# Three products instead of two while the stream comes in, and the sum of squares moved from GpSimd to ACT and DVE

## The chip, the cores and the metric

One core of one Trainium2 chip runs the whole program. The metric is device time in microseconds, the median of several executions. A separate profiled execution gives the page and the trace that are quoted.

## The reference

A two-layer decoder trunk on 512 tokens of 1024 numbers, in float32. Layer 0 mixes with a gated linear recurrence (HGRN2) in eight heads, layer 1 with differential attention; after each stands a gated feed-forward block with a short convolution. The change touches the very beginning of layer 0:

```python
def rmsnorm(x, g):
    x32 = x.astype(jnp.float32)
    y = x32 * lax.rsqrt(jnp.mean(x32 * x32, axis=-1, keepdims=True) + EPS)
    return (y * g.astype(jnp.float32)).astype(x.dtype)

def hgrn2_mixer(h, w_in, w_out, g_norm, lb):
    proj = h @ w_in
    q, f, i, g = jnp.split(proj, [HG_FDIM, 2 * HG_FDIM, 3 * HG_FDIM], axis=-1)
    q = jax.nn.silu(q)
    log_f = jnp.logaddexp(jnp.log(lb), jnp.log1p(-lb) + jax.nn.log_sigmoid(f))
    k = -jnp.expm1(log_f)
    ...
    o = rmsnorm(o, g_norm) * jax.nn.silu(g)
    return o @ w_out
```

Each head has four products with the normalised input: f (forget), q, i (the values, called V here) and g (the output gate). The mean square of x is needed for every token before any of them can be used; since it is a factor for a whole token, the products run on x times the gain, and the factor is applied to the result.

## The kernel before

Activations lie transposed: eight tiles x0 to x7 of 128 features by 512 tokens. Every float32 product is made of three matmuls (mm3, L99 to L104): an operand is split into a high part (ACT, L57 for weights, L60 for x) and a low part (DVE, L58 and L61), and high x high, low x high and high x low are added up. A product of one head's f, q or g is thus 8 k-tiles of 3 matmuls of 512 columns, 24 in all, into one PSUM bank of the tag mm, of which there are four. V is made for two heads at once from two weights of 512 KB (w_i), in four chunks of 128 tokens, each 24 matmuls of 256 columns into a bank of mm.

Weights come by SyncE's queue (SP, L79) into three staging buffers (wst), in the order in which the program issues them; SP waits at an issue until its buffer has been split. The split weights whi and wlo have three buffers each.

begin (L226 to L271) is written out by hand (manual_schedule) for TensorE, DVE, ACT and GpSimd. The x tiles and the first two weights (f and q of head 0), the latter in four pieces of 1, 2, 3 and 2 k-tiles, come in turns. For each k-tile x is split, then the pieces that have come, then three matmuls of f and three of q run. Beside it the sum of squares is made: GpSimd squares tiles 0 to 3 and adds them (L262, L265, L266), ACT squares tiles 4 to 7 (L243), DVE adds those (L245) and joins both sums (L268, L269).

Behind it come sums (L181: the sum over features, by TensorE with a tile of ones), rstd on DVE (L191 and L158 to L164, which ends in rcol) and TensorE's L186, which turns rcol into a tile rb that ACT copies (L198). V is evacuated with rcol (ACT, L320), f and q with rb (DVE, L327 and L337, fe and qe).

After begin the order of hgrn is not written by hand: a scheduler orders the instructions of each engine ahead of time, by what it thinks each lasts. The loop over heads has prep (from fe and qe to the decayed q and k of all levels, on DVE and ACT), values (V), intra (scores within a chunk: TensorE L412 to L426 into the bank at; transposes of k L434, copied by ACT L436 as kt; states kt x V L439; masks on DVE L457; readout products L479 and L481), gate (L486 to L489: g times rb is ge, its sigmoid sg, the product gg) and readout. gate(0) runs in the loop at head 2, on project(2), the product with weight number 2.

At head 2 bias_vector makes the table of relative biases for the attention much later: a matmul (L708), a subtraction on DVE (L709) and a write of 1024 rows of 383 numbers to a buffer in HBM, bdram, by SP's queue (L711). It stands among the weights on that queue.

Of the kernel before, what the change touches and what calls it, by code (L numbers as in the profile page):

```python
# [11 lines left out]
F32 = mybir.dt.float32  # L12
F32R = mybir.dt.float32r
I32 = mybir.dt.int32
AF = mybir.ActivationFunctionType
ALU = mybir.AluOpType
# [3 lines left out]
P = 128  # L20
T = 512
D = 1024
KD = D // P
# [11 lines left out]
class Trunk:  # L35
# [187 lines left out]
        return self.gains[:, which, n:n + 1]  # L223


    def begin(self, xs, acc, f_ps, q_ps):  # L226

        tc, nc, a = self.tc, self.nc, self.a
        v, s, pool = nc.vector, nc.scalar, nc.gpsimd
        raw = [self.wp.tile([P, 1024], F32, tag="wst", name="wst", bufs=3) for _ in range(2)]  # L230
        parts = [self.weight_tiles() for _ in range(2)]
        for k in range(KD):
            nc.sync.dma_start(self.x[k], a["x_t"][k])
            if k in PIECES:
                c = slice(k * P, PIECES[k] * P)
                for i in range(2):
                    nc.sync.dma_start(raw[i][:, c], a["w_fqg"][i][:, c])
        half = KD // 2
        sqs = [self.sp.tile([P, T], F32, tag="sq", name="sq", bufs=2) for _ in range(2)]
        acc2 = self.sp.tile([P, T], F32, tag="res", name="acc2", bufs=1)  # L240

        def squares(n):
            s.activation(acc2 if n == half else sqs[n % 2], self.x[n], AF.Square)  # L243
            if half < n < KD - 1:
                v.tensor_tensor(acc2, acc2, sqs[n % 2], ALU.add)  # L245

        with tc.manual_schedule(engines=ORDERED):
            warm = self.bank("at")
            for _ in range(WARM):
                nc.tensor.matmul(warm[:, 0:P], self.ones, self.ones, start=True, stop=True)  # L250
            for k in range(KD):
                xs.append(self.x_split(k, 0))
                if k in PIECES:
                    c = slice(k * P, PIECES[k] * P)
                    for w, (hi, lo) in zip(raw, parts):
                        self.split(w[:, c], hi[:, c], lo[:, c])
                for ps, w in zip((f_ps, q_ps), parts):
                    self.proj(ps, w, xs, [k])
                if k > half:
                    squares(k - 1)  # L260
                if k == 0:
                    pool.tensor_tensor(acc, self.x[0], self.x[0], ALU.mult)  # L262
                elif k < half:
                    sq = self.sp.tile([P, T], F32, tag="rbc", name="sqp")
                    pool.tensor_tensor(sq, self.x[k], self.x[k], ALU.mult)  # L265
                    pool.tensor_tensor(acc, acc, sq, ALU.add)  # L266
            squares(KD - 1)
            v.tensor_tensor(acc, acc, acc2, ALU.add)  # L268
            self.summed = v.tensor_tensor(acc, acc, sqs[(KD - 1) % 2], ALU.add).ins  # L269
        with tc.issue_after(self.last[0]), tc.issue_after(self.last[1]):  # L270
            self.setup_rest()  # L271

    def hgrn(self, xs, acc, on_tile):
        tc, nc, a, sp = self.tc, self.nc, self.a, self.sp
        v, s = nc.vector, nc.scalar
        with ExitStack() as ctx:
            hp = ctx.enter_context(tc.tile_pool(name="hgrn", bufs=1))
            self.banks(ctx, "hgrn", mm=(4, 1), at=(4, 1))
            f_ps, q_ps = self.bank(), self.bank()
            self.begin(xs, acc, f_ps, q_ps)  # L280
            rb, rc = self.rstd(self.sums(acc, "at"), "n0", "at")

            dl = hp.tile([P, NH], F32, tag="dl", name="dl")
# [14 lines left out]
            def big(tag, name, bufs):  # L298
                return hp.tile([P, T], F32, tag=tag, name=name, bufs=bufs)

            def project(n):
                w = self.weights(a["w_fqg"][n])
                ps = self.bank("mm")
                self.proj(ps, w, xs, range(KD))
                return ps

            def values(qt):
                ws = [self.weights(a["w_i"][qt, 0])]
                with tc.issue_after(self.summed):
                    ws.append(self.weights(a["w_i"][qt, 1]))  # L310
                vt = hp.tile([P, 4, 256], F32, tag="vt", name="vt", bufs=2)
                for j in range(4):
                    ps = self.bank("mm")
                    tk = slice(j * P, (j + 1) * P)
                    for k in range(KD):
                        hi, lo = ws[k // 4]
                        c = slice((k % 4) * 256, (k % 4) * 256 + 256)
                        self.mm3(ps[:, :256], (xs[k][0][:, tk], xs[k][1][:, tk]), (hi[:, c], lo[:, c]),
                                 k == 0, k == KD - 1)
                    s.activation(vt[:, j], ps[:, :256], AF.Identity, scale=rc[:, j:j + 1])  # L320
                return vt
# [162 lines left out]
            def gate(h, g_ps):  # L484
                ge, sg = big("tmp", "ge", 4), big("tmp", "sg", 4)
                v.tensor_tensor(ge, g_ps, rb, ALU.mult)  # L486
                s.activation(sg, ge, AF.Sigmoid)
                gg = big("gg", "gg", 2)
                v.tensor_tensor(gg, ge, sg, ALU.mult)  # L489
                return gg  # L490

            def keep(h, po):
                o = big("o", "o", 2)
                self.sq_add(oacc, po, h == 0)
                s.copy(o, po)
                return o

            def readout(h, o, gg):
                y = big("tmp", "y", 4)
                v.scalar_tensor_tensor(y, o, self.gain(6, h), gg, ALU.mult, ALU.mult)  # L500
                self.split(y, *ys[h])

            vt, pr, o = {}, {}, {}
            for h in range(NH):
                if h:
                    f_ps, q_ps = project(3 * h), project(3 * h + 1)
                pr[h] = prep(h, f_ps, q_ps)
                if h % 2 == 0:
                    vt[h // 2] = values(h // 2)
                if h:  # L510
                    o[h - 1] = keep(h - 1, intra(h - 1, vt[(h - 1) // 2], *pr.pop(h - 1)))
                if h > 1:
                    readout(h - 2, o[h - 2], gate(h - 2, project(3 * h - 4)))
                if h == 2:
                    self.bias_vector()
            gg = [gate(h, project(3 * h + 2)) for h in (NH - 2, NH - 1)]
# [732 lines left out]
```

## Time and profile before

| | us |
|---|---|
| median of 3 executions | 1283.47 (1282.53 to 1287.66) |
| profiled execution | 1283.88, its span 1282.0 |
| TensorE busy | 1246.9 |
| DVE busy | 869.2 |
| ACT busy | 567.9 |
| GpSimd busy | 111.1 |
| first product matmul starts | 4.95 |
| last matmul of f and q starts | 21.45 |
| head 0's first readout product (L479) | 65.63 |
| the bias matmul (L708) | 100.17 |
| the states of head 2 (L439) | 142.05 |

In a row of a timeline stand the start in us, the length in us, the engine, the line, the operation, out<-in, shape and count; in brackets the idle time ahead of it on its engine, and what ended that. Rows of waits have the total in us, how often, and the longest. A row of windows has a stretch and its length, the busy us and counts of TensorE, weight loads, DVE, ACT and GpSimd, then the granted clock, the DMA share and GB/s.

### The profile page before, as it was taken

The numbers are of one execution on the slowest core, as the hardware profiler recorded it, in microseconds if no ns is written. First come the engines' busy times: TensorE is split into PE (matmuls) and PEld (weight loads), VectorE is DVE, ScalarE is ACT, GpSimd is POOL, SyncE is SP. The second block draws the span as 40 slices with busy tenths as digits, with TensorE's granted clock in tenths as the row PEclk, the third lists the DMA queues.
The fourth block names the chain that finished last, engine by engine and source line by source line (L and its number), as shares of the span: only waits on it lengthen the run. The fifth ranks groups of instructions, "written<-read, shape, count | busy, mean of one in ns | idle before, by whom it ended". The sixth has DMA issues, their size and how long they took to land.

```text
span 1282.0 us, 18032 instructions
## 1 busy us (share of the span) xinstructions
PE 1246.9 (97%) x6994; PEld 1045.2 (82%) x6994; DVE 869.2 (68%) x1627; ACT 567.9 (44%) x986; POOL 111.1 (9%) x93
## 2 busy tenths in 40 slices
PE   8999899999999999999999899999999999999997
PEld 7888698778888888888878788798788888888886
DVE  7978689676877777533357888876687777762223
ACT  5554455454444444322235546554454444442221
POOL 3000000020000000001143432200200000000001
PEclk9999899999999999999999899999999999999998
DMA  6225322132333333233322221222232333333321
GB/s 208 83 85 81 102 67 84 50 115 83 99 99 99 99 99 99 82 100 91 97 76 83 74 67 58 66 83 67 89 107 96 92 96 97 99 91 90 95 86 66
DMA packets 37949, 115.35 MB, mean 90 GB/s; under 512 B 4032, under 2 KB 9448, under 8 KB 37864
## 3 DMA queue, kind: packets, MB, share of 16 engines
q1 hardware_dynamic: 36968, 113.29, 29.6%
q8 instruction: 55, 0.90, 0.3%
q10 hardware_dynamic: 896, 0.92, 0.2%
q14 instruction: 30, 0.25, 0.1%
HBM read 110.52 MB, written 3.67 MB: 89 GB/s over the span
## 4 chain that ended last, share of the span: by engine, by line
PE 53%; issue 30%; DVE 11%; ACT 3%; DMA 2%; POOL 0%; SPq 0%; POOLq 0%; ACTq 0%; DVEq 0%
PE mm L103 15%; PE mm L102 15%; PE mm L104 15%; DMA wst<-in_w_fqg_dram 2%; DVE wlo L759 1%; DVE kl L857 1%; PE po L1005 1%; DVE wlo L58 1%; ACT whi L756 1%; DVE sd L457 1%; DVE sc L964 1%; PE tp L992 1%; DVE qs L840 1%; ACT p L970 0%; ACT whi L57 0%
## 5 line engine op out<-in xcount | busy, mean ns | idle before, releaser
L102 PE MATMUL mm<-xh,whi 128*128 128x512 f32 x1008 | 399.6, 396 | 0.4 <-ACT whi L57 0.4
L103 PE MATMUL mm<-xl,whi 128*128 128x512 f32 x1008 | 396.4, 393 | 3.0 <-DVE xl L61 2.9
L104 PE MATMUL mm<-xh,wlo 128*128 128x512 f32 x1008 | 396.0, 393 | 1.1 <-DVE wlo L58 1.1
L58 DVE TENSOR_TENSOR wlo<-wst,whi 128x1024 fp32r<-128x1024 f32 (+2 forms) x182 | 215.7, 1189 | 165.8 <-ACT whi L57 163.4
L57 ACT CAST whi<-wst 128x1024 fp32r<-128x1024 f32 (+2 forms) x182 | 181.8, 1003 | 257.9 <-PE mm L103 192.4
L103 PEld LDWEIGHTS mm<-xl,whi 128*128 128x128 f32 x1008 | 191.0, 190 | 42.4 <-DVE xl L61 4.5
L104 PEld LDWEIGHTS mm<-xh,wlo 128*128 128x128 f32 x1008 | 190.7, 189 | 42.2 <-DVE wlo L58 2.3
L102 PEld LDWEIGHTS mm<-xh,whi 128*128 128x128 f32 x1008 | 191.0, 190 | 38.8 <-ACT whi L57 1.2
L102 PE MATMUL mm<-hh,whi 128*128 128x512 f32 (+1 forms) x374 | 142.8, 382 | 0.0
L103 PE MATMUL mm<-hl,whi 128*128 128x512 f32 (+1 forms) x374 | 142.6, 381 | 0.0
L104 PE MATMUL mm<-hh,wlo 128*128 128x512 f32 (+1 forms) x374 | 142.6, 381 | 0.0
L667 DVE TENSOR_TENSOR u<-mm,rbc_f 128x512 f32<-128x512 f32 x88 | 60.2, 688 | 73.4 <-PE mm L104 73.4
L147 POOL TENSOR_TENSOR acc<-acc,sq 128x512 f32<-128x512 f32 x18 | 26.7, 1482 | 664.2 <-ACT sq L146 664.1
L102 PEld LDWEIGHTS mm<-hh,whi 128*128 128x128 f32 x374 | 70.1, 188 | 15.2
L104 PEld LDWEIGHTS mm<-hh,wlo 128*128 128x128 f32 x374 | 70.1, 188 | 15.2
L103 PEld LDWEIGHTS mm<-hl,whi 128*128 128x128 f32 x374 | 70.1, 188 | 15.1
L669 ACT ACTIVATE c<-u,pack 128x512 f32<-128x512 f32 x88 | 71.5, 816 | 7.7 <-DVE u L667 4.0
L102 PE MATMUL mm<-whi,xh 128*128 128x256 f32 x256 | 73.8, 290 | 0.0
L103 PE MATMUL mm<-wlo,xh 128*128 128x256 f32 x256 | 72.5, 283 | 0.6 <-DVE wlo L759 0.6
L57 ACT CAST hh<-c 128x512 fp32r<-128x512 f32 x44 | 27.2, 619 | 102.9 <-DVE c L678 102.9
L104 PE MATMUL mm<-whi,xl 128*128 128x256 f32 x256 | 72.4, 283 | 0.0
L671 DVE SCALAR_TENSOR_TENSOR c<-u,pack,c 128x512 f32<-128x512 f32 x88 | 66.1, 752 | 2.7
(259 smaller groups left out, 1717.0 us busy)
## 6 DMA issues: line engine op xcount, KB each, us to landing
wst<-in_w_up_dram SPq DMA_DIRECT2D x88, 512.0 KB, 3.6
wst<-in_w_down_dram SPq DMA_DIRECT2D x32, 512.0 KB, 3.5
wst<-in_w_fqg_dram SPq DMA_DIRECT2D x22, 512.0 KB, 4.1
wst<-in_w_kq_dram SPq DMA_DIRECT2D x16, 512.0 KB, 3.6
wst<-in_w_down_dram SPq DMA_DIRECT2D x16, 384.0 KB, 3.2
wst<-in_w_i_dram SPq DMA_DIRECT2D x8, 512.0 KB, 4.2
wst<-in_w_ao_dram SPq DMA_DIRECT2D x8, 512.0 KB, 4.0
wst<-in_w_v_dram SPq DMA_DIRECT2D x8, 512.0 KB, 3.6
```

What stands on the lines that cost most here:

```text
L57: i = nc.scalar.copy(hi, x)
L58: j = nc.vector.tensor_tensor(lo, x, hi.bitcast(F32), ALU.subtract)
L102: mm(out, s[0], m[0], start=start, stop=False)
L103: mm(out, s[0], m[1], start=False, stop=False)
L104: mm(out, s[1], m[0], start=False, stop=stop)
L147: add = lambda engine=nc.vector: engine.tensor_tensor(acc, acc, sq, ALU.add)
L457: v.copy_predicated(dst, m, src)
L667: v.tensor_tensor(u[:, 2:], ps, rb, ALU.mult)
L669: s.activation(c, u[:, 2:], AF.Identity, bias=self.cb[:, layer, n:n + 1], scale=w(2))
L671: v.scalar_tensor_tensor(c, u[:, 0:T], w(0), c, ALU.mult, ALU.add)
L756: s.copy(me.w[0], me.st)
L759: v.tensor_tensor(me.w[1], me.st, me.w[0].bitcast(F32), ALU.subtract)
```

## The change

begin runs three products of head 0 (f, q and g) instead of two: three weights come in pieces, and per k-tile nine matmuls run. ACT squares all eight tiles (the first into acc), DVE makes the seven additions, and GpSimd does nothing there. gate(0) is computed right behind prep(0), and the loop at head 2 uses its result.

```diff
-    def begin(self, xs, acc, f_ps, q_ps):
+    def begin(self, xs, acc, products):
...
-        raw = [self.wp.tile([P, 1024], F32, tag="wst", name="wst", bufs=3) for _ in range(2)]
-        parts = [self.weight_tiles() for _ in range(2)]
+        raw = [self.wp.tile([P, 1024], F32, tag="wst", name="wst", bufs=3) for _ in products]
+        parts = [self.weight_tiles() for _ in products]
...
-        def squares(n):
-            s.activation(acc2 if n == half else sqs[n % 2], self.x[n], AF.Square)
-            if half < n < KD - 1:
-                v.tensor_tensor(acc2, acc2, sqs[n % 2], ALU.add)
+        sqs = [acc] + [self.sp.tile([P, T], F32, tag="sq", name="sq", bufs=2) for _ in range(KD - 1)]
+
+        def add(n):
+            return v.tensor_tensor(acc, acc, sqs[n], ALU.add)
...
-                for ps, w in zip((f_ps, q_ps), parts):
+                for ps, w in zip(products, parts):
                     self.proj(ps, w, xs, [k])
-                if k > half:
-                    squares(k - 1)
-                if k == 0:
-                    pool.tensor_tensor(acc, self.x[0], self.x[0], ALU.mult)
-                elif k < half:
-                    sq = self.sp.tile([P, T], F32, tag="rbc", name="sqp")
-                    pool.tensor_tensor(sq, self.x[k], self.x[k], ALU.mult)
-                    pool.tensor_tensor(acc, acc, sq, ALU.add)
-            squares(KD - 1)
-            v.tensor_tensor(acc, acc, acc2, ALU.add)
-            self.summed = v.tensor_tensor(acc, acc, sqs[(KD - 1) % 2], ALU.add).ins
+                s.activation(sqs[k], self.x[k], AF.Square)
+                if k > 1:
+                    add(k - 1)
+            self.summed = add(KD - 1).ins
...
-            f_ps, q_ps = self.bank(), self.bank()
-            self.begin(xs, acc, f_ps, q_ps)
+            f_ps, q_ps, g_ps = (self.bank() for _ in range(3))
+            self.begin(xs, acc, (f_ps, q_ps, g_ps))
...
                 pr[h] = prep(h, f_ps, q_ps)
+                if h == 0:
+                    gate0 = gate(0, g_ps)
...
-                    readout(h - 2, o[h - 2], gate(h - 2, project(3 * h - 4)))
+                    readout(h - 2, o[h - 2], gate(h - 2, project(3 * h - 4)) if h > 2 else gate0)
```

The scheduler orders everything behind begin anew. From there on the lines of hgrn stand 11 lower in the changed file and those of bias_vector 9 lower.

TensorE before, from the last matmul of q to the second pair of value chunks (mm_400, mm_426, mm_452 and mm_478 are the four chunks, the numbers tell tiles apart; whi_389 and whi_395 are the two halves of w_i, at_247 the sums, at_274 the tile rb):

```order
L104 MATMUL mm_91<-xh7_227,wlo_97 128x512
L102 MATMUL mm_400<-whi_389,xh0_128 128x256 [waits Activation_49]
L102 MATMUL mm_426<-whi_389,xh0_128 128x256
...
L102 MATMUL mm_400<-whi_395,xh4_190 128x256 [waits Activation_49]
L102 MATMUL mm_426<-whi_395,xh4_190 128x256
L181 MATMUL at_247<-ones_80,acc_82 128x1 [waits DVE_49]
...
L186 MATMUL at_274<-pack_243,rcol_n0_254 128x128 [waits DMAHW2_49,DVE_49]
...
L102 MATMUL mm_452<-whi_389,xh0_128 128x256 [waits Activation_49]
```

Two chunks run interleaved ahead of L186, with the sums among them. The same place after the change (mm_92 is g of head 0; mm_447, mm_473, mm_499 and mm_525 are the chunks):

```order
L104 MATMUL mm_92<-xh7_267,wlo_101 128x512
L181 MATMUL at_288<-ones_80,acc_82 128x1 [waits DVE_49]
L181 MATMUL at_288<-ones_80,acc_82 128x1 x3
L102 MATMUL mm_447<-whi_436,xh0_140 128x256 [waits Activation_49]
...
L186 MATMUL at_315<-pack_284,rcol_n0_295 128x128 [waits DMAHW5_49,DVE_49]
...
L102 MATMUL mm_473<-whi_436,xh0_140 128x256 [waits Activation_49]
...
L102 MATMUL mm_499<-whi_436,xh0_140 128x256 [waits DVE_49]
```

The sums come first, one chunk stands ahead of L186, and the third and fourth chunk wait for DVE, which reads f, q and g out of their banks.

SP before, around the bias table (wst_1803, wst_1844 and wst_1875 are weights of the heads 2 to 4, one after the other):

```order
L79 DMA wst_1579<-in_w_i_dram 128x1024 [waits DMAHW6_49,DVE_49]
L79 DMA wst_1585<-in_w_i_dram 128x1024 [waits DMAHW7_49,DVE_49]
L79 DMA wst_1803<-in_w_fqg_dram 128x1024 [waits DMAHW0_49,DVE_49]
L711 DMA bdram_1155<-bvec_1150 1024x1x383 [waits DVE_49]
L79 DMA wst_1844<-in_w_fqg_dram 128x1024 [waits DMAHW1_49,DVE_49]
L79 DMA wst_1875<-in_w_fqg_dram 128x1024 [waits DMAHW2_49,DVE_49]
```

and after (wst_1813, wst_1854 and wst_1885 are the same three weights):

```order
L79 DMA wst_1589<-in_w_i_dram 128x1024 [waits DMAHW1_49,DVE_49]
L79 DMA wst_1595<-in_w_i_dram 128x1024 [waits DMAHW2_49,DVE_49]
L79 DMA wst_1813<-in_w_fqg_dram 128x1024 [waits DMAHW3_49,DVE_49]
L79 DMA wst_1854<-in_w_fqg_dram 128x1024 [waits DMAHW4_49,DVE_49]
L702 DMA bdram_1165<-bvec_1160 1024x1x383 [waits DVE_49]
L79 DMA wst_1885<-in_w_fqg_dram 128x1024 [waits DMAHW5_49,DVE_49]
```

One weight more is issued ahead of the table. On ACT the casts of these weights stand ahead of kt, before:

```order
L57 CAST whi_1846<-wst_1844 128x1024 [waits DMAHW7_49,PE_49]
L320 ACTIVATE vt_1591<-mm_1670,rcol_n0_254 128x256 [waits PE_49]
L57 CAST whi_1877<-wst_1875 128x1024 [waits DMAHW0_49]
L395 COPY q128_1286<-q64_1278 128x4x64 [waits DVE_49,PE_49,Activation_49]
L357 COPY k4_1530<-k1_1512 128x128 [waits DVE_49]
L436 COPY kt_1762<-at_1758 128x384 [waits PE_49]
```

and after:

```order
L57 CAST whi_1856<-wst_1854 128x1024 [waits DMAHW1_49,PE_49]
L309 ACTIVATE vt_1601<-mm_1680,rcol_n0_295 128x256 [waits PE_49]
L57 CAST whi_1887<-wst_1885 128x1024 [waits DMAHW3_49]
L384 COPY q128_1296<-q64_1288 128x4x64 [waits DVE_49,PE_49,Activation_49]
L346 COPY k4_1540<-k1_1522 128x128 [waits DVE_49]
L373 COPY q16_1560<-r2_1544 128x32x4 [waits DVE_49,PE_49]
L425 COPY kt_1772<-at_1768 128x384 [waits PE_49]
```

The two casts stay ahead of kt, in the same places; k4's source k1 is made on DVE behind both low parts before, and between them after.

More of the change, by code (lines that the diff above doesn't have):

```diff
@@ L223, in gain @@
         return self.gains[:, which, n:n + 1]
-    def begin(self, xs, acc, f_ps, q_ps):
+    def begin(self, xs, acc, products):
         tc, nc, a = self.tc, self.nc, self.a
-        v, s, pool = nc.vector, nc.scalar, nc.gpsimd
-        raw = [self.wp.tile([P, 1024], F32, tag="wst", name="wst", bufs=3) for _ in range(2)]
-        parts = [self.weight_tiles() for _ in range(2)]
+        v, s = nc.vector, nc.scalar
+        raw = [self.wp.tile([P, 1024], F32, tag="wst", name="wst", bufs=3) for _ in products]
+        parts = [self.weight_tiles() for _ in products]
         for k in range(KD):
@@ L235, in begin @@
                 c = slice(k * P, PIECES[k] * P)
-                for i in range(2):
+                for i in range(len(products)):
                     nc.sync.dma_start(raw[i][:, c], a["w_fqg"][i][:, c])
-        half = KD // 2
-        sqs = [self.sp.tile([P, T], F32, tag="sq", name="sq", bufs=2) for _ in range(2)]
-        acc2 = self.sp.tile([P, T], F32, tag="res", name="acc2", bufs=1)
-        def squares(n):
-            s.activation(acc2 if n == half else sqs[n % 2], self.x[n], AF.Square)
-            if half < n < KD - 1:
-                v.tensor_tensor(acc2, acc2, sqs[n % 2], ALU.add)
+        sqs = [acc] + [self.sp.tile([P, T], F32, tag="sq", name="sq", bufs=2) for _ in range(KD - 1)]
+        def add(n):
+            return v.tensor_tensor(acc, acc, sqs[n], ALU.add)
         with tc.manual_schedule(engines=ORDERED):
```

## The prediction

> **What bounds the kernel now.** I read the first and second part of the page, then the waits of TensorE, then the timelines of the stages that the change touches.
>
> ```profile
> PE 1246.9 (97%) x6994; PEld 1045.2 (82%) x6994; DVE 869.2 (68%) x1627; ACT 567.9 (44%) x986; POOL 111.1 (9%) x93
> PE at L439 <- ACT kt L436: 5.3, 1, 5.3
> ```
>
> TensorE is busy for 97% of a span of 1282.0 us. No product is removed, so the time can only change where TensorE waits or runs at half clock. Outside the attention, the largest wait of TensorE is 5.3 us, once, at L439. There are two places to look at: the stream at the start, which the change rewrites, and this wait, 140 us in.
>
> The stream, in TensorE's timeline and the windows (a stretch and its length, then busy us with counts of PE, PEld, DVE, ACT, POOL, then the granted clock, DMA share and GB/s):
>
> ```profile
> 4.95 0.51 PE L102 MATMUL mm<-xh,whi 128*128 128x512 f32 x1 [0.18 <-ACT whi L57]
> 10.83 0.40 PE L102 MATMUL mm<-xh,whi 128*128 128x512 f32 x1
> 16.22 0.39 PE L102 MATMUL mm<-xh,whi 128*128 128x512 f32 x1
> 21.45 0.39 PE L104 MATMUL mm<-xh,wlo 128*128 128x512 f32 x1
> 21.68 0.40 PE L102 MATMUL mm<-whi,xh 128*128 128x256 f32 x2
> 8.00:10.00 2.00, 1.08 (x4) 0.57 (x4) 2.00 (x2) 1.30 (x2) 2.00 (x2) 1.00 0.82 268
> 10.00:12.00 2.00, 1.01 (x4) 0.30 (x2) 2.00 (x2) 1.16 (x4) 1.92 (x3) 0.94 1.05 391
> 12.00:14.00 2.00, 1.82 (x4) 1.49 (x5) 2.00 (x3) 2.00 (x4) 1.92 (x2) 0.50 1.07 395
> ```
>
> From 16.22 to 21.68 stand 24 matmuls, 0.2275 us each; one product is 24 of them, 5.46 us. Two products would need 10.9 us, but took from 4.95 to 21.68, 16.7 us: 5.8 us are gaps and half clock. DVE is full there, and TensorE waits for it. DVE's own rows say why:
>
> ```profile
> 7.77 2.67 DVE L58 TENSOR_TENSOR wlo<-wst,whi 128x256 fp32r<-128x256 f32 x2
> 10.36 3.21 DVE L61 SCALAR_TENSOR_TENSOR xl<-x,gains,xh 128x512 fp32r<-128x512 f32 x2
> 13.50 2.10 DVE L58 TENSOR_TENSOR wlo<-wst,whi 128x384 fp32r<-128x384 f32 x2
> 15.52 2.07 DVE L61 SCALAR_TENSOR_TENSOR xl<-x,gains,xh 128x512 fp32r<-128x512 f32 x3
> 17.51 0.75 DVE L58 TENSOR_TENSOR wlo<-wst,whi 128x256 fp32r<-128x256 f32 x2
> 13.11 1.61 POOL L266 TENSOR_TENSOR acc<-acc,sqp 128x512 f32<-128x512 f32 x1
> ```
>
> The same two 128x256 splits took 2.67 us while GpSimd squared and added, and 0.75 us after its last operation (13.11 to 14.72). Two xl took 3.21 us in that stretch, three took 2.07 us later. So GpSimd's part costs DVE 1.9 + 1.8 + about 1.1 (the 128x384 pair alone put at 1.0, a little above the 256 pair's 0.75) = 4.8 us.
>
> The wait at L439, in the chain of waits (start, length):
>
> ```profile
> 100.17 0.74 PE at L708 x2
> 109.35 27.74 DMA wst<-in_w_fqg_dram
> 137.16 1.04 ACT whi L57
> 138.48 1.04 ACT whi L57
> 139.54 1.23 DVE wlo L58
> 141.62 0.38 ACT kt L436
> 142.05 1.65 PE at L439 x6
> 101.52 0.83 SPq L711 DMA_DIRECT2D bdram<-bvec  x1
> wst<-in_w_fqg_dram SPq DMA_DIRECT2D x22, 512.0 KB, 4.1
> 140.00:150.00 10.00, 7.95 (x25) 6.59 (x26) 9.97 (x34) 4.60 (x11) 0.00 (x0) 0.66 0.34 105
> ```
>
> Such a weight lands in 4.1 us as a rule (the page's row of DMA issues), here in 27.74 us. Ahead of it stands the bias table (L711), issued at 101.52, right after the bias matmul of 100.17, and the weight comes 35.6 us after that issue. ACT's cast of this weight stands in front of kt on ACT, kt feeds L439, so TensorE's other work runs dry before L439. The wait costs 5.3 us, and the mean clock of 0.66 in the ten us after it some 3 us more.
>
> **The change, part by part.** *GpSimd's squares go.* DVE gets 4.8 us back. *ACT squares eight tiles, not four, DVE adds seven, not four:*
>
> ```profile
> ACT sq L243 <- DVE acc L245: 1.2, 1, 1.2
> 3.99 0.72 ACT L60 ACTIVATE xh<-x,gains 128x512 fp32r<-128x512 f32 x1 [1.98 <-DMA x<-in_x_t_dram]
> 13.22 0.61 ACT L243 ACTIVATE acc<-x 128x512 f32<-128x512 f32 x1
> 19.45 0.68 DVE L245 TENSOR_TENSOR acc<-acc,sq 128x512 f32<-128x512 f32 x1
> 14.35 0.39 ACT L57 CAST whi<-wst 128x256 fp32r<-128x256 f32 x1
> ```
>
> ACT gains 4 x 0.61 = 2.4 us of squares and a third weight's pieces, four times the 256 columns of 0.39 = 1.6 us; DVE gains 3 x 0.68 = 2.0 us of adds and 4 x 0.75 / 2 = 1.5 us of splits, against 4.8 us freed. Over the stream ACT then has eight xh (0.72 each), twelve casts and eight squares, 8 x 0.72 + 3 x 1.6 + 8 x 0.61 = 15.4 us, and DVE much the same: close to full, but under TensorE's 72 x 0.2275 = 16.4 us. The third weight adds 0.5 MB to the stream, 1.3 us at the 395 GB/s of the window 12 to 14; the last x tile waits longer than that for ACT already, so I cost it at nothing (1.3 us if that cover is gone).
>
> *The third product in the stream.* At best the stream is TensorE alone: 4.95 + 16.4 = 21.3. At worst all gaps stay: 21.68 + 5.46 = 27.1. The third tile's nine matmuls each start when x arrives; before, the third k-tile began at 10.83. I let it begin at 10.4 and run without gaps from there, 54 x 0.2275 = 12.3 us, so the stream ends at **22.75**, 1.07 later than now, with 5.46 us more done: a lead of 4.4 us. I take it near the lower end because the rows after 15.5, where GpSimd is silent, already show no gap.
>
> *Then the lead shrinks.* Three products hold three of the four PSUM banks called mm, and a value chunk needs one.
>
> ```profile
> 24.79 0.95 PE L181 MATMUL at<-ones,acc 128*128 128x1 f32 x8
> 27.76 0.16 DVE L164 SCALAR_TENSOR_TENSOR rcol_n<-rs 128x4 f32<-128x4 f32 x1
> 28.32 0.60 PE L186 MATMUL at<-pack,rcol_n 128*128 128x128 f32 x4
> 28.20 0.28 PE L104 MATMUL mm<-whi,xl 128*128 128x256 f32 x1
> 29.62 0.69 DVE L327 TENSOR_TENSOR fe<-mm,rbc_n 128x512 f32<-128x512 f32 x1 [1.70 <-ACT rbc_n L198]
> ```
>
> Before, two chunks (48 matmuls of 0.12 us) cover TensorE until 28.20 while DVE works out rcol. After, only one chunk (2.9 us) can run: sums from 22.75, 0.3 us for the split of w_i, and TensorE is dry at about 26.7. rcol comes at about 28.4 at the earliest, since three weight splits now stand around its chain on DVE. So **1.9 us** of new waiting (nothing if rcol comes 2 us sooner; 3.6 with a half-clock window behind it). The lead is 5.46 - 1.07 - 0.3 - 1.9 = 2.2 us.
>
> *The gate of head 0 moves ahead.* ge, gg and their sigmoid, 0.69 + 0.69 us on DVE, now stand inside prep(0):
>
> ```profile
> 84.56 0.69 DVE L486 TENSOR_TENSOR ge<-mm,rbc_n 128x512 f32<-128x512 f32 x1
> 86.80 0.69 DVE L489 TENSOR_TENSOR gg<-ge,sg 128x512 f32<-128x512 f32 x1
> 65.63 0.68 PE L479 MATMUL at<-scd,vt 128*128 128x128 f32 x4 [0.74 <-issue]
> ```
>
> The first readout product of head 0 (L479, 65.63) is where TensorE has waited for DVE (0.74). What DVE does up to there grows by 1.2 us of gate and fe comes 0.3 later, while some 0.6 us of other rows move behind it: ready at 66.6, 1.0 later. TensorE, with 3.54 us more matmul work placed before that point and a lead of 2.2, arrives at 64.88 + 3.54 - 2.2 = 66.2. So DVE decides, and TensorE leaves with 3.54 - 1.0 = **2.6 us of lead**, whatever the banks cost within 0.4.
>
> *The bias table.* By the bias matmul all 5.2 us of extra work is in front of it, so it runs at 100.17 + 5.2 - 2.6 = 102.8, and the table is issued at 104.1. On SP one more weight now passes ahead of it; the next, whose cast stands ahead of kt on ACT, is behind it and lands 35.6 us later, at 139.7. From landing to L439 took 137.16 to 142.05, 4.9 us, with two casts and DVE's k behind two splits; now k is ahead of the blocked split and one cast is left: cast 1.04, two or three small copies of about kt's length and kt itself 0.38, together 2.5. So L439 comes at **142.2, against 142.05**. From there the order is the same to the end.
>
> The sum: with a lead L at the bias matmul the end moves by 5.2 - L - 2.4 = +0.2 for L = 2.6. TensorE has done its products earlier and waits about 8 us where it waited 5.3. The profiled execution took 1283.88 us, span 1282.0 and 1.9 around it; the median of three is 1283.47, which I treat as the same. Forecast: **1284**, no change that a measurement can tell (it tells about 0.5%, 6.4 us).
>
> The bounds: L = 4.4 (no bank wait, DVE hidden) gives -1.6; L = 0 gives +2.8. The clock after the wait is about 3 us of loss now; a longer wait can move it by half a window either way, 1.7 us. That is 1280.6 to 1288.4.
>
> On the clock a page speaks. The granted clock fell to 0.50 in the window 12 to 14, after two windows in which TensorE was busy for 1.08 and 1.01 of 2.00. The Trainium skill, "TensorE: Matmul & The Clock Gate", section "Part 1: The HAM clock gate", says that the clock halves after at least one idle window of about 3.4 us; here half-busy was enough. By the page's rule the 1.9 us of bank waiting would cost no clock, and the sum stays 1284; by the row it may cost 1.7 us more there, which DVE's bound at L479 mostly swallows.
>
> **The rivals.** *A, the transfer does not take the gain back.* If the weight that kt waits for is not held as long behind the table, because one more is ahead, the lead of 2.6 remains and the wait shrinks with it. For it: the one weight that passes the table can be split, and k of the next head made, before the wait. Against: the next weight stands right behind the table, and the table takes its 35.6 us from its own issue. Half of the lead kept gives 1282, all of it 1281. If the wait at L439 vanished altogether, 5.3 and 3 us of clock go too: 1273.
>
> *B, slower: the stream is bound by ACT and DVE.* Both hold about 15 us of work in 17 us, and ACT's square waits for DVE's add because there are two sq tiles. If the stream ends after 25.2, the lead is 5.46 - 3.5 - 2.2 = -0.2 before the first gate, and DVE starts fe late by the same 3 us, so the bias matmul and with it the table come 5.2 + 2 later: the end moves by +4.8, and with one more half-clock window of 3.4 us at half loss by +6.5: 1290. For it: the wait of 1.2 us of sq for the add exists already (first of the rows of ACT and DVE above). Against: DVE's list is 1 us shorter than now. It decides from 25.2 on.
>
> *C, the change does not do what it says: DVE was not slowed by GpSimd but by something else in that stretch, say DMA writes at 391 to 395 GB/s.* Then the slow rows stay, the stream ends near 27 and the time goes as in B, 1290. Against: the last xl rows and the 0.75 us pair have a quiet GpSimd and also less DMA, so the trace cannot part the two. The Trainium skill, "SBUF — State Buffer", section "SBUF: two separate sides", says that a DVE operation with two SBUF inputs and a GpSimd operation that reads SBUF exclude each other, and that DMA and engines do not contend; the 2.67 and 0.75 us agree, and by that rule C falls away.
>
> **How the numbers follow.** Forecast 0.68 (1284, its own range 1281 to 1288); A with part or all of the lead 0.15 (1281 to 1282); A with the wait gone 0.04 (1273); B 0.09 and C 0.04 (1290). The range takes the bounds of the unknown costs and stops short of B's far end and of 1273: 1280 to 1289. Faster by over 0.5% is only the wait gone, 0.04; slower by over 0.5% (1289.9 and more) is about half of B and C and a little of an unknown, 0.08; within it 0.88.
>
> **What would show it.** The last product matmul of the stream near 22.75 and splits of 128x256 pairs near 0.75 (not 2.67): the stream. A wait of TensorE near 27 to 28.5, ended by rcol: the banks. The first readout product near 66.6. The bias matmul near 102.8, the table issued near 104, a weight landing near 139.7, a wait of about 8 us at kt, then 142.2. If L439 starts before 139.5 or after 144, the table's part is wrong; if the stages after it move against L439, my claim that nothing else changes is.

## The result, and the profile after

The changed kernel takes 1286.98 us (median of 20 runs), the kernel before 1284.05 (20 runs): 1.0020 times as long, 95% interval 1.0012 to 1.0028. Ratios here and below leave out single slow runs, one of these 20 among them (2502.51 us). By the ratio that is some 2.6 us slower, by the medians 2.9: within the half per cent that the forecast called no change, but clear of zero, and above the forecast of 1284. The profiled execution of the changed kernel took 1284.07 us, the shortest of its 20, so its rows tell where time goes, while the size of the loss is read from the medians.

First the page and the waits of TensorE of the changed kernel, to compare with 1246.9 us and the 5.3 us at L439:

```profile
PE 1244.2 (97%) x6994; PEld 1043.1 (81%) x6994; DVE 868.0 (68%) x1633; ACT 571.0 (45%) x993; POOL 101.2 (8%) x86
PE at L428 <- ACT kt L425: 7.9, 1, 7.9
PE at L186 <- DVE rcol_n L164: 1.5, 1, 1.5
```

The wait for kt grew from 5.3 to 7.9 us, and a wait for rcol is new. The stream itself became as fast as hoped. DVE's groups from 4 to 20 us, before (line, operation, shape, count, busy us, mean ns):

```profile
L61 DVE SCALAR_TENSOR_TENSOR xl<-x,gains,xh 128x512 fp32r<-128x512 f32 x8 | 7.7, 994 | 5.6 <-ACT xh L60 5.6
L58 DVE TENSOR_TENSOR wlo<-wst,whi 128x256 fp32r<-128x256 f32 (+2 forms) x8 | 6.1, 791 | 0.1
```

and after:

```profile
L61 DVE SCALAR_TENSOR_TENSOR xl<-x,gains,xh 128x512 fp32r<-128x512 f32 x8 | 6.0, 749 | 6.4 <-ACT xh L60 6.3
L58 DVE TENSOR_TENSOR wlo<-wst,whi 128x256 fp32r<-128x256 f32 (+2 forms) x12 | 4.5, 420 | 0.6 <-ACT whi L57 0.5
```

Twelve splits of the same three shapes take less than eight did. Before, w_i was issued while the stream ran, and its first split was done before the sums (rows of SP and DVE):

```profile
10.61 7.67 SPq L79 DMA_DIRECT2D wst<-in_w_i_dram  x2
20.19 1.22 DVE L58 TENSOR_TENSOR wlo<-wst,whi 128x1024 fp32r<-128x1024 f32 x1
22.79 2.48 DVE L58 TENSOR_TENSOR wlo<-wst,whi 128x1024 fp32r<-128x1024 f32 x2
```

What follows the stream, in the timelines of TensorE, SP, DVE and ACT of the changed kernel:

```profile
22.84 0.39 PE L104 MATMUL mm<-xh,wlo 128*128 128x512 f32 x1
23.07 0.95 PE L181 MATMUL at<-ones,acc 128*128 128x1 f32 x8
17.92 0.81 SPq L79 DMA_DIRECT2D wst<-in_w_i_dram  x2
23.22 1.23 DVE L58 TENSOR_TENSOR wlo<-wst,whi 128x1024 fp32r<-128x1024 f32 x1 [1.67 <-ACT whi L57]
24.09 1.05 ACT L57 CAST whi<-wst 128x1024 fp32r<-128x1024 f32 x1 [0.91 <-PE at L181]
25.18 1.23 DVE L58 TENSOR_TENSOR wlo<-wst,whi 128x1024 fp32r<-128x1024 f32 x1 [0.73 <-ACT whi L57]
26.32 0.15 DVE L191 TENSOR_SCALAR rms_n<-at 128x4 f32<-128x4 f32 x1
26.39 1.23 DVE L58 TENSOR_TENSOR wlo<-wst,whi 128x1024 fp32r<-128x1024 f32 x1
29.30 0.16 DVE L164 SCALAR_TENSOR_TENSOR rcol_n<-rs 128x4 f32<-128x4 f32 x1
29.52 0.65 PE L186 MATMUL at<-pack,rcol_n 128*128 128x128 f32 x4 [1.49 <-DVE rcol_n L164]
30.83 0.69 DVE L316 TENSOR_TENSOR fe<-mm,rbc_n 128x512 f32<-128x512 f32 x1 [1.36 <-ACT rbc_n L198]
68.19 0.68 PE L468 MATMUL at<-scd,vt 128*128 128x128 f32 x4 [0.90 <-issue]
```

The sums run from 23.07, but DVE's first step on them (L191) comes at 26.32, since two splits stand ahead of it, and a third stands between it and the rest of its chain. All three staging buffers went to f, q and g, so w_i, whose first half was issued at 10.61 before, is issued at 17.92, and ACT's cast ahead of the first split waits for its transfer. Staging is not all: f, q and g hold the three split buffers too, and the cast ahead of the second split (24.09) waits for TensorE by the profile. fe is 1.2 us later than before, and the first readout product 2.6 us.

At the bias table, in the timelines of TensorE (the bias matmul from the chain of waits), SP and ACT:

```profile
104.42 0.74 PE at L699 x2
105.77 0.84 SPq L702 DMA_DIRECT2D bdram<-bvec  x1
141.34 1.05 ACT L57 CAST whi<-wst 128x1024 fp32r<-128x1024 f32 x1 [12.67 <-DMA wst<-in_w_fqg_dram]
143.12 0.47 ACT L425 COPY kt<-at 128x384 f32<-128x384 f32 x1
143.65 1.65 PE L428 MATMUL at<-vt,kt 128*128 128x128 f32 x6 [7.88 <-ACT kt L425]
```

The table goes out 4.25 us later than before. The cast of the weight behind it starts 35.6 us after that issue, as before, and kt's product 2.3 us after the cast's start. It comes at 143.65 against 142.05.

### The profile page after: what moved, and what is told of

The parts are those of the page before. It is cut to its first block, busy times and chain, and to the rows that moved or that the text cites. A ratio compares the mean times of both kernels' runs of the same rounds, so it can differ in the third digit from the quotient of the medians.

```text
span 1282.1 us, 18046 instructions
## 1 busy us (share of the span) xinstructions
PE 1244.2 (97%) x6994; PEld 1043.1 (81%) x6994; DVE 868.0 (68%) x1633; ACT 571.0 (45%) x993; POOL 101.2 (8%) x86
## 4 chain that ended last, share of the span: by engine, by line
PE 54%; issue 30%; DVE 10%; ACT 3%; DMA 2%; POOL 0%; SPq 0%; POOLq 0%; ACTq 0%; DVEq 0%
PE mm L102 16%; PE mm L103 16%; PE mm L104 15%; DMA wst<-in_w_fqg_dram 2%; DVE wlo L750 1%; PE po L996 1%; DVE wlo L58 1%; DVE kl L848 1%; DVE sd L446 1%; ACT whi L747 1%; PE tp L983 1%; DVE sc L955 1%; ACT whi L57 1%; PE sc L103 0%; PE sc L102 0%
## 5 line engine op out<-in xcount | busy, mean ns | idle before, releaser
L58 DVE TENSOR_TENSOR wlo<-wst,whi 128x1024 fp32r<-128x1024 f32 (+3 forms) x185 | 213.5, 1159 | 166.7 <-ACT whi L57 164.5
L57 ACT CAST whi<-wst 128x1024 fp32r<-128x1024 f32 (+3 forms) x185 | 182.4, 992 | 262.9 <-PE mm L103 192.0
L147 POOL TENSOR_TENSOR acc<-acc,sq 128x512 f32<-128x512 f32 x18 | 26.7, 1482 | 678.9 <-ACT sq L146 678.7
```

The source lines that it names most:

```text
L57: i = nc.scalar.copy(hi, x)
L58: j = nc.vector.tensor_tensor(lo, x, hi.bitcast(F32), ALU.subtract)
L147: add = lambda engine=nc.vector: engine.tensor_tensor(acc, acc, sq, ALU.add)
```

## The experiments

"First readout" below is head 0's first readout product (L479 before, L468 after), "states" the product that waits for kt (L439, L428). Ratios are to the kernel before, run beside each.

**The table on another queue (e1, e2).** The same line is edited in the changed kernel (e1) and in the kernel before (e2):

```diff
-        nc.sync.dma_start(self.bdram, u[0:NH, 0:383]...
+        nc.scalar.dma_start(self.bdram, u[0:NH, 0:383]...
```

> The changed kernel with the write of the bias table issued on ACT's queue instead of SP's. Theory 1 (the weight that kt waits for is held because it stands behind the table on SP's queue): the weight lands in under 12 us instead of 27.7, the wait of TensorE for kt falls from 7.9 us to under 3, and the time falls by 4 to 10 us, to 1277 to 1283. Rival (the 16 DMA engines are busy with the table whatever its queue): the weight still needs over 25 us, the wait stays within 1 us of 7.9, and the time within 2 us of 1287.

> The kernel before with the same edit: table on ACT's queue. Theory 1: the wait of 5.3 us for kt falls under 2, the time falls by 4 to 9 us from 1284, to 1275 to 1280; and the changed kernel with the same edit is then not slower than this one but about 1 us faster, since its lead of 0.95 us at the bias matmul is no longer taken back. Rival: the wait stays within 1 us of 5.3, and the time at 1284; the changed kernel stays 2 to 3 us slower.

Measured: 1278.05 us for e1 (0.9963, 0.9951 to 0.9976) and 1275.98 for e2 (0.9939, 0.9926 to 0.9951). The wait for kt is gone from both, so the weight's place behind the table made that wait. It is not all that held the weight: in e1 it lands 19.4 us after its issue, against 27.7 in the changed kernel and under 12 expected, so the table slows it from another queue too. The second part of e2's expectation failed: with the table out of the way the change still does not win. TensorE's waits in the changed kernel with this edit, and three of its rows (this profiled execution, 1282.57 us, was the slowest of e1's nine):

```profile
PE at L408 <- issue: 4.1, 1, 4.1
30.36 0.16 DVE L164 SCALAR_TENSOR_TENSOR rcol_n<-rs 128x4 f32<-128x4 f32 x1
69.24 0.68 PE L468 MATMUL at<-scd,vt 128*128 128x128 f32 x4 [0.89 <-issue]
106.81 0.80 ACTq L702 DMA_DIRECT2D bdram<-bvec  x1
```

rcol came another microsecond later than in the changed kernel, though begin is the same in both, and the table's issue is 5.3 us behind the 101.52 of e2: all of the extra work in front of it, so no lead is left in this execution. A second wait stands at L408, in the middle of a group of equal products, for nothing that the profile shows.

**The gate later (e5).** The g product stays in the stream, its ge and gg are held back on DVE until head 0's last mask:

```diff
-                if h == 0:
-                    gate0 = gate(0, g_ps)
...
+                if h == 1:
+                    with tc.issue_after(self.masked):
+                        gate0 = gate(0, g_ps)
```

> The changed kernel with gate(0) on DVE held back until the last mask of head 0 (the product g still runs in the stream). Theory 1 (DVE sets the first readout product, so the gate's two operations count there): that product starts at 66.8 to 67.1 instead of 68.19, the bias matmul at 103.2 instead of 104.42, kt's product at 142.4 instead of 143.65, and the time falls by about 1.2 us. Rival (TensorE's own lateness sets it: banks and value chunks): the readout product stays within 0.3 us of 68.19.

Measured: 1285.05 us (1.0014, 1.0005 to 1.0022). The rows:

```profile
30.48 0.16 DVE L164 SCALAR_TENSOR_TENSOR rcol_n<-rs 128x4 f32<-128x4 f32 x1
32.00 0.69 DVE L316 TENSOR_TENSOR fe<-mm,rbc_n 128x512 f32<-128x512 f32 x1 [1.36 <-ACT rbc_n L198]
67.97 0.68 PE L468 MATMUL at<-scd,vt 128*128 128x128 f32 x4
```

In this execution rcol was 1.2 us later again, and hid what the edit does: read alone, 67.97 speaks for the rival. From fe to the first readout are 35.97 us here and 37.36 in the changed kernel, 1.4 less, as much as the gate's two operations of 0.69 us, and the wait of 0.90 us ahead of it is gone. So the gate does count on DVE, and the start of that stretch moves from run to run. The time does not show the gain of 1.2 us: this interval overlaps that of the change alone. The states came at 145.76, later than expected, because the weight landed 37 us after the table's issue instead of 35.6; why is open.

**rcol first (e6).** DVE's split of the second half of w_i, and those of later f, q and g weights, are held until rcol is done; their transfers are not:

```diff
-                w = self.weights(a["w_fqg"][n])
+                st = self.stage(a["w_fqg"][n])
+                with tc.issue_after(rooted):
+                    w = self.weight_split(st)
...
-                with tc.issue_after(self.summed):
-                    ws.append(self.weights(a["w_i"][qt, 1]))
+                st = self.stage(a["w_i"][qt, 1])
+                with tc.issue_after(rooted):
+                    ws.append(self.weight_split(st))
```

> The changed kernel with the chain that ends in rcol ahead of DVE's splits of the second half of w_i and of the next f weight. Theory 1 (rcol is late because two splits of 1.2 us stand ahead of and within its chain, and all of prep(0) is late with it): rcol by 26.7 instead of 29.46, fe by 29.0 instead of 30.83, the first readout product by 66.5 instead of 68.19, kt's product by 142.0 instead of 143.65, and the time falls by about 1.8 us. Rival (the third PSUM bank starves the value chunks, rcol or not): TensorE waits as long in other places before head 1's products, and the readout product stays within 0.5 us of 68.19.

Measured: 1283.02 us (0.9999, 0.9990 to 1.0008), an interval that lies wholly under that of the change alone. Its rows:

```profile
26.11 0.16 DVE L164 SCALAR_TENSOR_TENSOR rcol_n<-rs 128x4 f32<-128x4 f32 x1
28.47 0.69 DVE L320 TENSOR_TENSOR fe<-mm,rbc_n 128x512 f32<-128x512 f32 x1
66.98 0.68 PE L472 MATMUL at<-scd,vt 128*128 128x128 f32 x4
104.44 0.84 SPq L706 DMA_DIRECT2D bdram<-bvec  x1
142.32 1.65 PE L432 MATMUL at<-vt,kt 128*128 128x128 f32 x6 [7.88 <-ACT kt L429]
```

rcol 3.2 us earlier, fe 2.4, first readout 1.2, table 1.3, states 1.3, time back to that of before. TensorE has no wait ahead of its first readout any more, which would be why half of what fe gains stops there. The rival falls: the third bank is still taken, and the wait at L186 is 0.4 us here. The third PSUM bank only turned a late rcol into waiting of TensorE.

**Half of the change (e3, e4).** e3 has two products and the new squares, e4 three products and the old squares (GpSimd tiles 0 to 3). e3 against the changed kernel (gate(0) is back in the loop), then e4 against the kernel before (begin takes a list of products; gate(0) as in the changed kernel):

```diff
-            f_ps, q_ps, g_ps = (self.bank() for _ in range(3))
-            self.begin(xs, acc, (f_ps, q_ps, g_ps))
+            f_ps, q_ps = self.bank(), self.bank()
+            self.begin(xs, acc, (f_ps, q_ps))
```

```diff
-                for ps, w in zip((f_ps, q_ps), parts):
+                for ps, w in zip(products, parts):
```

> Two products in the stream as before, squares on ACT and sums on DVE as after, no GpSimd. It tells the two halves of the change apart. Theory 1 (GpSimd slowed DVE in the stream): the pair of 128x256 splits at 0.75 to 0.95 us instead of 2.67, the last product matmul near 18 to 19.5 instead of 21.45, rcol and fe 1 to 2 us earlier, the first readout product 64 to 64.6 instead of 65.63; kt's product earlier by the same 1 to 1.6 us, time 1282 to 1283. Rival (arrivals set the stream): the last product matmul stays within 0.5 us of 21.45 and the time at 1284.

> Three products in the stream, but the squares as before: GpSimd tiles 0 to 3, ACT 4 to 7. The other half of the change. Theory 1 (GpSimd slows DVE in the stream, and DVE then feeds three weights' splits): the 128x256 splits near 1.3 us each instead of 0.47, the last product matmul after 24 instead of 22.8, fe after 31.5, the first readout product after 69, kt's product after 144.5; time 1288 to 1292. Rival (GpSimd costs nothing once TensorE sets the pace): the last product matmul within 0.5 us of 22.8 and the time within 1 us of 1287.

Measured: e3 1283.79 us (0.9995, 0.9986 to 1.0005), e4 1288.11 (1.0027, 1.0016 to 1.0038). Rows of DVE, TensorE and SP in e3:

```profile
7.71 0.75 DVE L58 TENSOR_TENSOR wlo<-wst,whi 128x256 fp32r<-128x256 f32 x2
64.71 0.68 PE L468 MATMUL at<-scd,vt 128*128 128x128 f32 x4 [0.64 <-issue]
100.59 0.83 SPq L700 DMA_DIRECT2D bdram<-bvec  x1
142.67 1.65 PE L428 MATMUL at<-vt,kt 128*128 128x128 f32 x6 [6.84 <-ACT kt L425]
```

Without GpSimd the early pair takes 0.75 us (2.67 before), and first readout and table come 0.9 us earlier; rcol, at 27.04, gains 0.7 us, less than expected. The last product starts at 22.30, not at 18 to 19.5, because the scheduler put 24 matmuls of the value chunks (17.59 to 21.37) among the last of the products, so the end of the stream is no measure here. The states come 0.6 later nevertheless, with a wait of 6.8 us, and the time is that of before: what is won ahead of the table is lost behind it. The first of the two weights was cast at 136.21, again 35.6 us after the table; the second waited for its transfer until 139.09, and why it took so long is open. In e4 the trio of such splits took 3.01 us again:

```profile
7.53 3.01 DVE L58 TENSOR_TENSOR wlo<-wst,whi 128x256 fp32r<-128x256 f32 x3
24.96 0.39 PE L104 MATMUL mm<-xh,wlo 128*128 128x512 f32 x1
69.13 0.68 PE L479 MATMUL at<-scd,vt 128*128 128x128 f32 x4 [1.01 <-issue]
```

The stream ends 2.1 us later than with the new squares, the first readout 0.9 later, kt's product at 144.98. The time, 1.0027 against 1.0020, cannot be told from the whole change's.

**Four staging buffers (e8, e9).** In the changed kernel (e8) and in the kernel before (e9):

```diff
-        st = self.wp.tile([P, 1024], F32, tag="wst", name="wst", bufs=3)
+        st = self.wp.tile([P, 1024], F32, tag="wst", name="wst", bufs=4)
```

> The changed kernel with four staging buffers instead of three. w_i is then issued in the stream again, and the weight whose cast stands ahead of kt is issued ahead of the table. Theory 1 (rcol is late because three weights land late; the wait at kt is that weight behind the table): w_i issued near 12 instead of 17.9, rcol by 28.5 instead of 29.3, the first readout product by 67.4, no wait at kt (7.9 to under 1), and a time of 1272 to 1276. Rival (the table slows all transfers of the DMA engines, in front of it or not): a wait of over 3 us stays near kt, 1280 or more.

> The kernel before with four staging buffers. One weight passes the table, the one behind it is still the second whose cast stands ahead of kt, as in the changed kernel. Theory 1: table issued at 101.5, that weight lands 35.6 us later at 137.1, kt's product 2.4 us after it at 139.6 instead of 142.05, and the time falls by about 2.5 us, to 1281 to 1282. Rival (the wait is set by the mass of the transfers): kt's product within 0.7 us of 142.05.

Measured: 1274.18 us for e8 (0.9942, 0.9921 to 0.9963), 1280.54 for e9 (0.9973, 0.9964 to 0.9982). In e8 the first readout is at 67.16, as the theory has it, and so are w_i and rcol (SP and DVE):

```profile
11.76 6.71 SPq L79 DMA_DIRECT2D wst<-in_w_i_dram  x2
23.05 2.36 DVE L58 TENSOR_TENSOR wlo<-wst,whi 128x1024 fp32r<-128x1024 f32 x2 [1.35 <-ACT whi L57]
28.30 0.16 DVE L164 SCALAR_TENSOR_TENSOR rcol_n<-rs 128x4 f32<-128x4 f32 x1
```

Only the second and third split gain by the early weight, though. The first starts at 23.05, against 23.22, because its cast starts at 21.96 even here, just when f's last matmul, which started at 21.72, makes room for the next. That fits a cast that waits for f's split buffer; no run has a fourth of these. The wait for kt is gone from both profiles, and another, told of in the last section, stands in its place: 7.1 us in e8's profiled execution, which took 1283.15 us, far above its median, and in e9's

```profile
PE at L419 <- issue: 6.8, 1, 6.8
```

so e9's time is within 0.5 us of the theory's, and its way there does not agree: its states came at 144.81, not at 139.6.

**A shorter write of the table (e12).** The changed kernel, with the 8 vectors made twice, so that 16 partitions write 64 rows each instead of 8 partitions 128:

```diff
+        two = tab[0:32, NH + 384:3 * NH + 384]
+        nc.scalar.copy(two.rearrange("p (h a) -> p h a", a=2), tab[0:32, 0:NH].unsqueeze(2).broadcast_to([32, NH, 2]))
...
-        nc.sync.dma_start(self.bdram, u[0:NH, 0:383].unsqueeze(1).broadcast_to([NH, P, 383]))
+        nc.sync.dma_start(self.bdram.rearrange("h (a p) d -> (h a) p d", a=2),
+                          u[0:2 * NH, 0:383].unsqueeze(1).broadcast_to([2 * NH, P // 2, 383]))
```

> The changed kernel with the same table of 1024 rows written from 16 partitions of 64 rows each instead of 8 partitions of 128 (the 8 vectors are made twice, by one small ACT copy and a matmul of 16 columns). It tests whether the length of the table's write sets the wait. Theory 1 (half of the DMA engines carry the write now, their share is 0.44 to 0.49 while it runs; 16 partitions use all): the write takes some 18 us instead of 33 to 35, the held weight lands under 20 us after the table's issue instead of 35.6, the wait for kt (7.9) goes, and the time is 1274 to 1278, with the lead of 0.95 us kept. Rival (the write is limited by its packets to HBM, not by the number of engines): the weight still lands 30 us or more after the issue, and the time stays within 2 us of 1287.

Measured: 1276.52 us (0.9942, 0.9929 to 0.9956). The window from 110 to 120 of the changed kernel, then that of e12, with its rows of SP and ACT and the states:

```profile
110.00:120.00 10.00, 10.00 (x69) 9.23 (x68) 10.00 (x32) 4.87 (x11) 0.00 (x0) 1.00 0.55 75
110.00:120.00 10.00, 10.00 (x70) 9.29 (x69) 10.00 (x37) 3.94 (x9) 0.00 (x0) 1.00 0.91 98
106.48 0.67 SPq L704 DMA_DIRECT2D bdram<-bvec  x1
128.24 1.04 ACT L57 CAST whi<-wst 128x1024 fp32r<-128x1024 f32 x1
135.42 0.83 PE L428 MATMUL at<-vt,kt 128*128 128x128 f32 x6
```

The DMA share while the table runs is 0.91 instead of about half (0.55 in the changed kernel, a weight included), the write lands 18.0 us after its issue, the cast of the weight starts 21.8 us after the table's issue without waiting for it, the wait for kt is gone, and the states come 8.2 us earlier, although the table itself goes out later. The scheduler also ordered the instructions anew, so that the weight is issued 1.1 us behind the table instead of 7.8; it lands 18.9 us after that, 2 us behind the table, so the table still sets when it lands. So it is the length of this write, on the queue of the weights, that decides when the states run. The Trainium skill, "DMA: Bandwidth & Descriptors", section "Why a DMA increments its semaphore by 16 and not by 1", says that a transfer uses the largest number of DMA engines, up to 16, that divides the slowest dimension of both its sides; 8 and 16 rows in that place, with shares of about half and of 0.91, agree.

**The remedies together (e7, e10, e11).** rcol first with the table on ACT's queue (e7), with four buffers (e10), with both (e11), all in the changed kernel:

> The changed kernel with both edits: rcol's chain ahead of the two splits, and the table on ACT's queue. Theory 1 (the two losses are the late rcol and the table, and they add): rcol near 26.1, the first readout product near 67.0, no wait over 3 us near 130 to 143, and a time below the kernel before with the table on ACT (0.9939 of before) by the lead of 2.2 us: 1273 to 1276. Rival (the changed order has a further loss behind the table, as the wait of 4.1 us at L408 with the table on ACT's queue suggests): 1277 to 1279.

> The changed kernel with rcol's chain ahead of the two splits and with four staging buffers. Theory 1 (late rcol and the held weight are the two losses): rcol by 26.2, the first readout product by 66.8, no wait for kt, time 1272 to 1275 as with the table on ACT's queue. Rival (TensorE's wait at L408 without a releaser, seen with four buffers, is regular): 1279 to 1283.

> All three edits: rcol's chain first, four staging buffers, table on ACT's queue. Theory 1: nothing is left to gain from the second of two remedies for the same wait, so within 2 us of the better of the two, 1272 to 1275. Rival (each remedy removes a part): 1268 to 1271.

Measured: e7 1273.82 us (0.9928, 0.9908 to 0.9949), e10 1276.31 (0.9940, 0.9920 to 0.9960), e11 1272.74 (0.9909, 0.9893 to 0.9926). All three beat both kernels; their intervals overlap among them and with e2's, which e11's only touches. e7 and e11 came out as their theories had it; e10's median lies between its theory and its rival, and its rcol (26.74) and first readout (67.59) came 0.5 and 0.8 us later than expected. In e7 neither kt nor the unexplained wait holds TensorE for 3 us: the states stand at 133.75.

## Why the prediction was right or wrong

The forecast of no change holds within its half per cent, and its reason, that the stream's gain does not reach the end, holds too. But the sum had +0.2 us where +2.6 were measured, and the interval keeps that apart from nothing. That the profiled execution of the changed kernel took just 1284 us is luck: it is the shortest of 20.

*The stream* was right: the last product ends where the sums follow, at 23.07, against the 22.75 forecast, and the clock stayed at 1.00 where it had been 0.50. GpSimd was the cause of DVE's slow rows: 791 ns per split became 420, e3 takes its part away with two products and e4 gives it back with three, and rival C falls. The Trainium skill, "SBUF — State Buffer", section "SBUF: two separate sides", gives this exclusion as a rule; the pair of 2.67 us with GpSimd and of 0.75 us without it, in the same place of the stream, agree with it.

*The banks*: the wait at L186 was 1.5 us (1.9 forecast), its cause as described, but both its ends came over 1 us later than forecast (26.7 and 28.4).

*The step that was mis-sized* is rcol. It was put at 28.4 "at the earliest", and fe 0.3 us later than before; rcol came at 29.5 and fe 1.2 us later. I had counted the three splits on DVE but not that they wait for weights which are issued 7 us later than before, since g's weight holds the third staging buffer. e8, where they are issued early, has rcol at 28.30, about as forecast, so this wait is worth 1.0 us of it. The rest is the splits' place ahead of the chain: e6, which takes them out of it with w_i issued as late as ever, has rcol at 26.11 and takes back the whole loss of 2.6 us. Of the four executions profiled with an unchanged begin, rcol started at 29.08 (e12) and 29.30 (the changed kernel) in two that were among the fastest of their kernels, and at 30.36 (e1) and 30.48 (e5) in two among the slowest. So the loss varies, and the profiled execution of the changed kernel had a small one; that this makes up the difference between it and the median is likely, not shown.

*The gate* was mis-sized as well: from fe to the first readout DVE takes 37.36 us, 36.01 before. That is 1.35 us more, where 1.2 less 0.6 was forecast; the 0.6 us that were to move behind it did not. The prediction took the 0.74 us at L479 for a wait for DVE, while the row names no releaser; that this wait goes in e5 and e6 agrees with its reading. With fe, that gives 68.19 instead of 66.6, and a lead at the bias matmul of 5.2 - 4.25 = 0.95 us instead of 2.6.

*The table* was right: 35.6 us from its issue to the weight, 2.3 us (2.5 forecast) to kt's product. The formula 5.2 - L - 2.4 gives +1.8 for L = 0.95, and the trace has +1.6 at that point; for L = 0 the text had +2.8. By head 3's readout products the two profiled executions were only 0.9 us apart, and at the end 0.1; the profiles don't explain that last part, and the medians do not show it. In the window from 720 to 730 us the granted clock was 0.74 in the execution before and 0.91 in the one after, which goes the way of the difference.

*Rivals.* A (the lead survives) did not come about; e1 shows that moving the table alone does not bring it back. B (ACT and DVE bind the stream) did not either: its end state, no lead at the table, was nearly reached by another way. As for the clock, after the 1.5 us wait at L186 the changed kernel kept a clock of 1.00, but in e1, where TensorE was busy for 0.98 of the 2 us from 24, it fell to 0.50 in the window 28 to 30: the half-clock price named for this wait is sometimes paid. Nor does a half-busy TensorE always cost the clock, as the prediction read from one row: e4 kept 1.00 from 8 to 14 us with 1.09 and 1.33 of 2.00 busy in the first two windows, and the changed kernel kept it with 0.51 busy from 28 to 30.

What three products are worth once rcol and the table are out of the way stays open: e7 (0.9928) and e2 (0.9939) cannot be told apart, and the kernel before with rcol first was not tried.

## What to carry to other kernels

When a transfer or a product is pulled into the start of a program, look at what it takes the place of: here a staging buffer, a split buffer and a PSUM bank. Look also at where a short, critical chain then stands: here, on DVE, behind long splits that wait for those buffers. Ask of each wait behind the change when it is released: this one ended some 36 us after a slow write was issued, so work moved ahead of that write only made the wait longer. Shorten such a write by spreading it over more partitions, put it on a queue that nothing urgent shares, or let the urgent loads pass it.

## What was not expected of the hardware

A wait of TensorE for nothing that the profile shows turned up in the middle of one group of equal small matmuls (L408, L412 or L419), at the time of the table's write. In e1, e8, e9, e10 and e11 it lasted 3.9 to 7.4 us. Here e10's, in the waits and in TensorE's timeline:

```profile
PE at L412 <- issue: 7.4, 1, 7.4
135.84 0.45 PE L412 MATMUL at<-q,k 128*32 128x16 f32 x17 [7.35 <-issue]
```

In the trace's list of transfers, the queue of instructions (q8) moves a block of 16 KB near 119 to 125 us in the kernels without this wait; in those with it, that block is missing there and comes at 131.9 (e1), 132.9 (e8), 134.6 (e9), 133.5 (e10) and 129.1 us (e11), and TensorE resumes 2.3 to 2.5 us after its start. In e2 it comes at 128.3, and the wait is 0.4 us. That TensorE waits for its own instructions there is argued from this order, not shown by an experiment. The times suggest that it does not happen in every execution: of e10's runs six took 1272.1 to 1273.3 us and five 1279.3 to 1283.0, and the profiled one, 1282.13, had the wait; none of the six was profiled. The gain of four buffers would then be smaller on average than at best.
